# Attention: both heads of a tile multiply with v as a pair, in two column tiles of TensorE, with one PSUM bank and one evacuation

## The chip, the cores and the metric

The kernel runs on one core of a Trainium2 chip. The metric is the time of one execution on the device, in microseconds (us), and lower is better. Three runs of the kernel before gave 2673.93, 2676.56 and 2682.19 us, so the median is 2676.56 us.

## The reference, cut to what matters

The program is a stack of four layers over 1040 positions (16 meta tokens and 1024 of the sequence) with a model width of 1024: attention, mLSTM, HGRN2, attention. Layers 0 and 3 are sliding-window attention with 16 query heads of 64, four key/value heads and a window of 128 positions, computed in blocks of 128 queries against the block before and the block itself. The change touches the last line of this cut alone, in which the probabilities `p` meet the values `vv`:

```python
s = jnp.einsum('bnqhgd,bnkhd->bnhgqk', qb, kk) * (A_HD ** -0.5)
s = jnp.where(mask[None, :, None, None], s, -jnp.inf)
m = jnp.maximum(s.max(axis=-1), sink)
e = jnp.exp(s - m[..., None])
p = e / (e.sum(axis=-1) + jnp.exp(sink - m))[..., None]
o = jnp.einsum('bnhgqk,bnkhd->bnqhgd', p, vv)
...
return (o * jax.nn.silu(z.astype(jnp.float32))).astype(u.dtype) @ w_out
```

## The kernel before

Activations lie transposed: features on the 128 partitions, positions along the free axis, in three chunks of 400, 384 and 256 columns that hold blocks 0 to 3, 4 to 6, and 7 and 8. Block 0 is the 16 meta tokens alone. Projections run in three products of split operands each (`proj`, L255 and L300 for v, `proj_out`, L338), and they are most of the program.

In an attention layer (`layer_a`) the 16 heads stand in eight tiles `t` of two heads each. The two heads of a tile belong to the two key/value heads of a pair, so their 64 columns of v lie side by side: `V[kb][:, gcol : gcol + 128]` holds both. The attention of a tile is cut into *units*: block 0 alone, blocks 1 and 2, block 3, blocks 4 and 5, block 6, blocks 7 and 8, each once for each head `hh`. That makes 96 units in layer 0, and 80 in layer 3, which needs no output for the meta tokens and leaves block 0 out. Each unit goes through three steps:

- `S_step` (L583 to L623): two products of q and k for each block into a PSUM bank (L609, L610), then the mask and the maximum on VectorE (L614), the exponential with its sum on ScalarE (L618), and the division on VectorE (L620, L623) into the tile `Sm`.
- `T_step` (L625 to L640): TensorE transposes the probabilities, a 128x128 piece at a time (L634), and ScalarE copies them to SBUF as `Pt` (L640, or L637 for block 0).
- `V_step` (L642 to L660): for each block and each of its two key blocks one product in fp32 (L656), with 128 columns of v held in the array and `Pt` streamed through it. Each head has a PSUM bank of its own (`R["po", hh]`). All 128 output rows are computed, those of the other head too, and only the head's own 64 are copied out by ScalarE after the last unit of a chunk (L660):

```python
pe.matmul(po[:, q0 - c0 : q0 - c0 + nq], V[kb][:kn, gcol : gcol + P], Pt[:kn, u, ki, :nq],
          start=(ki == 0), stop=(ki == len(kbs) - 1))
```

In the trace each fp32 product of L656 stands as two weight loads and two matmuls, called passes here.

The order of TensorE's work is written out by hand. `mixers` (L662 to L673) lists the steps: in iteration k come the v step of unit k-4, the transposes of unit k-2 and the scores of unit k. So the two heads of a tile follow each other as single units. `weave` (L55) then mixes this list with the projections that are due (q of the next tile, the gate of the tile before, the output product of a pair of tiles): it takes the next element from the list that has had the smaller share of its total cost so far. The costs are TensorE nanoseconds given by hand: 427, 213 and 218 per block of a unit for the three steps, while a projection's part is its columns at 2.4 a nanosecond. `Sm` and `Pt` have two buffers each. The instructions of the other engines are ordered by priority, and those of the attention steps stand 40 ahead (`hi`, L357).

All PSUM tiles share eight banks (L144). The gate's projection for tile t (`gate_proj`, L432) multiplies into the row that L660 wrote.

Layer 2 (HGRN2) matters to the prediction for one reason: its `level_mm` (L1086 to L1108) already holds 32 columns of fp32 in the array for each product and writes the results to 32 PSUM partitions at a time, several products side by side (L1097, L1107).

Of the kernel before, what the change touches and what calls it, by code (L numbers as in the profile page):

```python
# [15 lines left out]
P = 128  # L16
# [13 lines left out]
def blk(b):  # L30
    return (0, NMETA) if b == 0 else (NMETA + P * (b - 1), P)
# [11 lines left out]
KT_LAG = 500.0  # L43
NORM_AT = (4000.0, 0.7), (5000.0, 0.5), (8000.0, 0.5)
Y_LAST, Y_EARLY, Y_AHEAD = 3, 8, 2500.0
T_LAG, V_LAG = 2, 4
PARTS = 2, 2, 2
FIRST = 0.3, 0.9, 0.3, 0.7
D_Q = 2000.0, 4000.0, 6000.0
# [21 lines left out]
def flat(groups):  # L71
    return [x for grp in groups for x in grp]
# [38 lines left out]
def hybrid_kernel(ctx: ExitStack, tc: tile.TileContext, ins, out, layers=(0, 1, 2, 3)):  # L111
    nc = tc.nc
    v, s, g, pe, sp = nc.vector, nc.scalar, nc.gpsimd, nc.tensor, nc.sync
# [11 lines left out]
    def nm(x):  # L125
        ctr[0] += 1
        return f"{x}{ctr[0]}"

    def row():
        return rpool.tile([P, T], F32, tag="r", name=nm("r"), bufs=ROWS)  # L130
# [10 lines left out]
    def small(w):  # L141
        return tpool.tile([P, w], F32, tag=f"s{w}", name=nm("s"), bufs=12 if w < 8 else 4)

    def psum(tag, bufs):  # L144
        return ps.tile([P, 512], F32, tag="p", name=nm(tag), bufs=8)
# [211 lines left out]
    def hi(fn):  # L357
        def f():
            with tc.high_priority(offset=PRIO):
                fn()  # L360

        return f
# [78 lines left out]
    def layer_a(i, j, first, last, fin):  # L441
        win, wout = ins["a_win"][j], ins["a_wout"][j]
        chunks = LAST_CHUNKS if last else CHUNKS
        R = {}
# [13 lines left out]
        order = {}  # L458
# [106 lines left out]
        V = {}  # L565
# [7 lines left out]
        def mixer(t):  # L573
            units = []
            for n, us in enumerate((((0,), (1, 2), (3,)), ((4, 5), (6,)), ((7, 8),))):
                if last and n == 0:
                    us = us[1:]
                for k, u in enumerate(us):
                    for hh in range(2):
                        units.append(dict(t=t, n=n, unit=u, hh=hh, first=k == 0, last=k == len(us) - 1))  # L580
            return units

        def mixers():  # L583
            def S_step(w):
                t = w["t"]
                mix, cons = R["mix"], R["cons"]
                unit, hh, n = w["unit"], w["hh"], w["n"]
                q, (kh, kl) = R["q", t, n][hh], R["k", t // 4][hh]
                c0 = chunks[n][0]
                nu, nq = len(unit), blk(unit[0])[1]  # L590
                head = (2 * (t // 4) + hh) * 4 + t % 4
                sink = cons[:nq, 2 + head : 3 + head]
                S = psum("pm", 2).rearrange("p (u k) -> p u k", u=2)
                w["Sm"] = Sm = mix.tile([P, 2, 257], F32, tag="Sm", name=nm("Sm"), bufs=2)
                st, den = small(2), small(2)
                w["geo"] = geo = []
                for u, b in enumerate(unit):
                    q0 = blk(b)[0]
                    if b == 0:
                        k0, kbs = 0, ((0, 0, 16),)  # L600
                    elif b == 1:
                        k0, kbs = 0, ((0, 0, 16), (1, 16, 128))
                    else:
                        k0, kbs = q0 - P, ((b - 1, 0, 128), (b, 128, 128))
                    nk = sum(z[2] for z in kbs)
                    geo.append((q0, nk, kbs))
                    kw = nk if b == 0 else 256
                    qb, kb = slice(q0 - c0, q0 - c0 + nq), slice(k0, k0 + kw)
                    pe.matmul(S[:nq, u, :kw], q[:, qb], kh[:, kb], start=True, stop=False)  # L609
                    pe.matmul(S[:nq, u, :kw], q[:, qb], kl[:, kb], start=False, stop=True)  # L610
                for u, b in enumerate(unit):
                    nk, mo = geo[u][1], {0: 128, 1: 112}.get(b, 0)
                    g.tensor_copy(Sm[:nq, u, nk : nk + 1], sink)
                    v.tensor_tensor_reduce(Sm[:nq, u, :nk], S[:nq, u, :nk], R["masks"][:nq, P + mo : P + mo + nk],  # L614
                                           -1.0, sink, ALU.add, ALU.min, st[:nq, u : u + 1])
                for u in range(nu):
                    nk = geo[u][1]
                    s.activation(Sm[:nq, u, : nk + 1], Sm[:nq, u, : nk + 1], AF.Exp, scale=-1.0,  # L618
                                 bias=st[:nq, u : u + 1], accum_out=den[:nq, u : u + 1])
                v.reciprocal(den[:nq, :nu], den[:nq, :nu])  # L620
                for u in range(nu):
                    nk = geo[u][1]
                    v.tensor_scalar(Sm[:nq, u, :nk], Sm[:nq, u, :nk], den[:nq, u : u + 1], None, op0=ALU.mult)  # L623

            def T_step(w):  # L625
                unit, geo, Sm = w["unit"], w["geo"], w["Sm"]
                nu, nq = len(unit), blk(unit[0])[1]
                pt = psum("pt", 1).rearrange("p (u k q) -> p u k q", u=2, k=2)
                w["Pt"] = Pt = R["mix"].tile([P, 2, 2, P], F32, tag="Pt", name=nm("Pt"), bufs=2)
                for u in range(nu):  # L630
                    q0, nk, kbs = geo[u]
                    for ki, (kb, ko, kn) in enumerate(kbs):
                        kn = kn if unit[u] == 0 else P
                        pe.transpose(pt[:kn, u, ki, :nq], Sm[:nq, u, ko : ko + kn], ident[:nq, :nq])  # L634
                full = [u for u in range(nu) if unit[u]]
                if not full:
                    s.copy(Pt[:NMETA, 0, 0, :nq], pt[:NMETA, 0, 0, :nq])  # L637
                else:
                    f0, f1 = full[0], full[-1] + 1
                    s.copy(Pt[:, f0:f1], pt[:, f0:f1])  # L640

            def V_step(w):  # L642
                unit, geo, Pt, hh, n, t = w["unit"], w["geo"], w["Pt"], w["hh"], w["n"], w["t"]
                nq = blk(unit[0])[1]
                if w["first"]:
                    if ("o", t) not in R:
                        R["o", t] = row()
                    R["po", hh] = psum("po", 1)
                po = R["po", hh]
                c0, cn = chunks[n]  # L650
                gcol = P * (t // 4)
                for u in range(len(unit)):
                    q0, nk, kbs = geo[u]
                    for ki, (kb, ko, kn) in enumerate(kbs):
                        kn = kn if unit[u] == 0 else P
                        pe.matmul(po[:, q0 - c0 : q0 - c0 + nq], V[kb][:kn, gcol : gcol + P], Pt[:kn, u, ki, :nq],  # L656
                                  start=(ki == 0), stop=(ki == len(kbs) - 1))
                if w["last"]:
                    hs = slice(64 * hh, 64 * hh + 64)
                    s.copy(R["o", t][hs, c0 : c0 + cn], po[hs, :cn])  # L660

            units = flat(mixer(t) for t in range(8))  # L662
            segs = [[] for _ in range(9)]
            for k in range(len(units) + V_LAG):
                seg = units[k]["t"] if k < len(units) else 8
                for lag, cost, fn in ((V_LAG, 427, V_step), (T_LAG, 213, T_step), (0, 218, S_step)):
                    if 0 <= k - lag < len(units):
                        w = units[k - lag]
                        step = [cost * len(w["unit"]), hi(lambda w=w, fn=fn: fn(w)), None]
                        segs[seg].append(step)  # L670
                        if fn is S_step and w["last"]:
                            order["S", w["t"], w["n"]] = step
            return segs  # L673

        zc = {t: gate_proj(win[12 + t], lambda t=t: R["o", t], chunks) for t in range(8)}
# [15 lines left out]
        if first:  # L691
            q0, qfin0 = qg[0]
# [4 lines left out]
        head[0].insert(0, [0.0, enter, None])  # L697
        body = []
        segs = mixers()
        for t in range(8):  # L700
            parts = [([], hang)]
# [18 lines left out]
        for t in range(1, 8):  # L720
            for n in range(3):
                at = [id(z) for z in body]
                q = at.index(id(order["q", t, n])) if id(order["q", t, n]) in at else -1
                k = at.index(id(order["S", t - 1, n]))
# [577 lines left out]
    ahead, k = 0.0, 0  # L1302
# [5 lines left out]
    k = 0  # L1308
# [125 lines left out]
```

## Time and profile before

| what | value |
|---|---|
| median of three runs | 2676.56 us |
| span of the profiled execution, first to last instruction | 2674.6 us |
| TensorE matmul busy | 2627.9 us, 98% of the span |
| VectorE busy | 1892.1 us, 71% |
| ScalarE busy | 1682.6 us, 63% |
| GpSimd busy | 151.8 us, 6% |
| v steps run in | 83 to 455 us and 2254 to 2624 us |

The span is 2.0 us shorter than the median run. In the profile's rows PE is TensorE's matmul, PEld its weight load, DVE VectorE, ACT ScalarE, POOL GpSimd and SP SyncE. A form such as `128*64 128x128` reads: rows by columns held in the array, then partitions by elements streamed through it. Matmuls overlap in the array, so the time from one start to the next says what one costs, and its duration does not.

### The profile page before, as it was taken

The numbers are of one execution on the slowest core, as the hardware profiler recorded it, in microseconds if no ns is written. First come the engines' busy times: TensorE is split into PE (matmuls) and PEld (weight loads), VectorE is DVE, ScalarE is ACT, GpSimd is POOL, SyncE is SP. The second block draws the span as 40 slices with busy tenths as digits, with TensorE's granted clock in tenths as the row PEclk, the third lists the DMA queues.
The fourth block names the chain that finished last, engine by engine and source line by source line (L and its number), as shares of the span: only waits on it lengthen the run. The fifth ranks groups of instructions, "written<-read, shape, count | busy, mean of one in ns | idle before, by whom it ended". The sixth has DMA issues, their size and how long they took to land.

```text
span 2674.6 us, 55510 instructions
## 1 busy us (share of the span) xinstructions
PE 2627.9 (98%) x20896; PEld 2535.8 (95%) x20896; DVE 1892.1 (71%) x5335; ACT 1682.6 (63%) x4301; POOL 151.8 (6%) x545
## 2 busy tenths in 40 slices
PE   7999999999999999999999999999999999999999
PEld 6999999999999999999999999899999999999999
DVE  6776767974747474747464688988888987677776
ACT  6767677565454545454544757878676857768683
POOL 1000000000000000000000000101000110000010
PEclk9999999999999999999999999999999999999999
DMA  4211111011111111111111101111111011111102
GB/s 133 60 38 49 41 49 38 17 65 56 40 56 40 56 40 56 40 56 40 56 40 49 56 26 41 33 34 33 41 33 38 29 59 49 56 43 48 46 25 87
DMA packets 74044, 126.67 MB, mean 47 GB/s; under 512 B 11552, under 2 KB 26016, under 8 KB 73776
## 3 DMA queue, kind: packets, MB, share of 16 engines
q1 hardware_dynamic: 73776, 123.13, 14.5%
q8 instruction: 165, 2.70, 0.4%
q14 instruction: 103, 0.84, 0.1%
HBM read 108.24 MB, written 4.26 MB: 42 GB/s over the span
## 4 chain that ended last, share of the span: by engine, by line
PE 82%; DVE 11%; ACT 4%; issue 1%; DMA 1%; POOL 0%; SPq 0%; DVEq 0%; ACTq 0%; POOLq 0%
PE pj L255 39%; PE pj L338 15%; PE pj L300 10%; PE po L656 4%; PE pt L634 2%; PE po L862 1%; PE pm L609 1%; PE pa L532 1%; PE pm L610 1%; PE pa L876 1%; DVE t L408 1%; PE po L864 1%; DVE ul L189 1%; DVE X L1084 1%; DVE X L1082 1%
## 5 line engine op out<-in xcount | busy, mean ns | idle before, releaser
L255 PE MATMUL pj<-uh,wh 128*128 128x384 f32 (+2 forms) x2592 | 898.5, 347 | 3.8 <-ACT uh L188 3.8
L255 PE MATMUL pj<-ul,wh 128*128 128x384 f32 (+2 forms) x2592 | 836.3, 323 | 3.1 <-DVE ul L189 2.8
L255 PE MATMUL pj<-uh,wl 128*128 128x384 f32 (+2 forms) x2592 | 834.3, 322 | 0.1
L255 PEld LDWEIGHTS pj<-uh,wh 128*128 128x128 f32 x2592 | 491.9, 190 | 23.3 <-issue 6.1
L255 PEld LDWEIGHTS pj<-ul,wh 128*128 128x128 f32 x2592 | 492.5, 190 | 14.6 <-DVE ul L189 5.9
L255 PEld LDWEIGHTS pj<-uh,wl 128*128 128x128 f32 x2592 | 491.5, 190 | 0.4 <-DVE wl L189 0.4
L300 PE MATMUL pj<-wh,uh 128*128 128x256 f32 x896 | 269.0, 300 | 0.0
L189 DVE TENSOR_TENSOR wl<-wr,wh 128x512 fp32r<-128x512 f32 x336 | 228.4, 687 | 51.9 <-ACT wh L188 48.9
L341 DVE TENSOR_TENSOR x<-x,pj 128x384 f32<-128x384 f32 (+2 forms) x480 | 235.4, 510 | 38.1 <-PE pj L338 36.4
L188 ACT CAST wh<-wr 128x512 fp32r<-128x512 f32 x337 | 202.5, 616 | 94.7 <-PE pj L338 31.8
L338 PE MATMUL pj<-yh,wh 128*128 128x384 f32 (+2 forms) x768 | 254.1, 331 | 0.0
L300 PE MATMUL pj<-wh,ul 128*128 128x256 f32 x896 | 252.8, 282 | 0.0
L300 PE MATMUL pj<-wl,uh 128*128 128x256 f32 x896 | 252.7, 282 | 0.0
L338 PE MATMUL pj<-yl,wh 128*128 128x384 f32 (+2 forms) x768 | 247.0, 322 | 3.2 <-DVE yl L189 3.2
L338 PE MATMUL pj<-yh,wl 128*128 128x384 f32 (+2 forms) x768 | 246.2, 321 | 0.0
L428 DVE SCALAR_TENSOR_TENSOR t<-pj,t 128x384 f32<-128x384 f32 (+2 forms) x192 | 98.9, 515 | 108.6 <-ACT t L427 106.6
L618 ACT ACTIVATE Sm<-Sm,s 128x257 f32<-128x257 f32 (+2 forms) x272 | 131.2, 484 | 69.3 <-DVE s L614 67.1
L300 PEld LDWEIGHTS pj<-wh,uh 128*128 128x128 f32 x896 | 169.5, 189 | 2.4
L300 PEld LDWEIGHTS pj<-wl,uh 128*128 128x128 f32 x896 | 169.7, 189 | 2.1
L429 ACT ACTIVATE t<-t 128x384 f32<-128x384 f32 (+2 forms) x240 | 117.7, 490 | 85.5 <-DVE t L428 84.7
L300 PEld LDWEIGHTS pj<-wh,ul 128*128 128x128 f32 x896 | 169.7, 189 | 0.0
L614 DVE CUSTOM_DVE_ANT_0 Sm<-pm,masks,cons 128x256 f32<-128x256 f32 (+2 forms) x272 | 115.9, 452 | 68.4 <-PE pm L610 63.7
(218 smaller groups left out, 5266.4 us busy)
## 6 DMA issues: line engine op xcount, KB each, us to landing
wr<-in_b_win SPq DMA_DIRECT2D x128, 256.0 KB, 2.7
wr<-in_a_win SPq DMA_DIRECT2D x80, 256.0 KB, 2.7
wr<-in_c_win SPq DMA_DIRECT2D x64, 256.0 KB, 2.7
r<-rowsd SPq DMA_DIRECT2D x16, 520.0 KB, 5.7
wr<-in_a_wout SPq DMA_DIRECT2D x32, 256.0 KB, 2.8
wr<-in_b_wout SPq DMA_DIRECT2D x32, 256.0 KB, 2.7
t<-t SPq DMA_DIRECT2D x96, 48.0 KB, 1.9
wr<-in_c_wout SPq DMA_DIRECT2D x16, 256.0 KB, 2.7
```

Of the source, the lines that this page charges most:

```text
L188: s.copy(h, src)
L189: v.tensor_tensor(l, src, h.bitcast(F32), op=ALU.subtract)
L255: pe.matmul(acc[:, :cn], a[:, k, :], b[:, k, c0 : c0 + cn], start=(k == 0 and i == 0), stop=(k == KT - 1 and i == 2))
L300: pe.matmul(acc[:cn, :256], a[:, k, c0 : c0 + cn], m[:, kk, :], start=(k == 0 and i == 0), stop=(k == KT - 1 and i == 2))
L338: pe.matmul(acc[:, :cn], a[:, k, mc], b, start=(k == 0 and i == 0), stop=(k == 1 and i == 2))
L341: v.tensor_tensor(x[:, m, c0 : c0 + cn], x[:, m, c0 : c0 + cn], acc[:, :cn], op=ALU.add)
L428: v.scalar_tensor_tensor(a[:, :cn], z, 0.0, a[:, :cn], op0=ALU.min, op1=ALU.subtract)
L429: s.activation(a[:, :cn], a[:, :cn], AF.Exp)
L614: v.tensor_tensor_reduce(Sm[:nq, u, :nk], S[:nq, u, :nk], R["masks"][:nq, P + mo : P + mo + nk], -1.0, sink, ALU.add, ALU.min, st[:nq, u : ...
L618: s.activation(Sm[:nq, u, : nk + 1], Sm[:nq, u, : nk + 1], AF.Exp, scale=-1.0, bias=st[:nq, u : u + 1], accum_out=den[:nq, u : u + 1])
L634: pe.transpose(pt[:kn, u, ki, :nq], Sm[:nq, u, ko : ko + kn], ident[:nq, :nq])
L656: pe.matmul(po[:, q0 - c0 : q0 - c0 + nq], V[kb][:kn, gcol : gcol + P], Pt[:kn, u, ki, :nq], start=(ki == 0), stop=(ki == len(kbs) - 1))
```

## The change

The v step now takes a pair, both heads of a unit. For each block and key block the two products follow each other: head 0's holds the 64 columns of v of its own head and writes to PSUM partitions 0 to 63, head 1's holds the next 64 columns and writes to partitions 64 to 127 of the same bank. Nothing is computed that isn't needed. One ScalarE copy of 128 partitions replaces two of 64. The number of products stays. The order of the steps changes with it: an iteration holds the v step of pair k-2, then for each head in turn the transposes of pair k-1 and the scores of pair k. The cost given to the weave for a pair's v step is 470 per block, where the two single steps had 427 each.

```diff
-T_LAG, V_LAG = 2, 4
...
-                    R["po", hh] = psum("po", 1)
-                po = R["po", hh]
+                    R["po"] = psum("po", 1)
+                po = R["po"]
...
-                        pe.matmul(po[:, q0 - c0 : q0 - c0 + nq], V[kb][:kn, gcol : gcol + P], Pt[:kn, u, ki, :nq],
-                                  start=(ki == 0), stop=(ki == len(kbs) - 1))
+                        for hh in range(2):
+                            vc = P * (t // 4) + 64 * hh
+                            pe.matmul(po[64 * hh : 64 * hh + 64, q0 - c0 : q0 - c0 + nq], V[kb][:kn, vc : vc + 64],
+                                      ws[hh]["Pt"][:kn, u, ki, :nq], start=(ki == 0), stop=(ki == len(kbs) - 1))
                 if w["last"]:
-                    hs = slice(64 * hh, 64 * hh + 64)
-                    s.copy(R["o", t][hs, c0 : c0 + cn], po[hs, :cn])
+                    s.copy(R["o", t][:, c0 : c0 + cn], po[:, :cn])
...
             units = flat(mixer(t) for t in range(8))
+            pairs = [units[k : k + 2] for k in range(0, len(units), 2)]
             segs = [[] for _ in range(9)]
-            for k in range(len(units) + V_LAG):
-                seg = units[k]["t"] if k < len(units) else 8
-                for lag, cost, fn in ((V_LAG, 427, V_step), (T_LAG, 213, T_step), (0, 218, S_step)):
...
+            for k in range(len(pairs) + 2):
+                seg = pairs[k][0]["t"] if k < len(pairs) else 8
+                v2, t1, s0 = (pairs[j] if 0 <= j < len(pairs) else None for j in (k - 2, k - 1, k))
+                if v2:
+                    put(seg, 470, V_step, v2, len(v2[0]["unit"]))
+                for hh in range(2):
+                    if t1:
+                        put(seg, 213, T_step, t1[hh], len(t1[hh]["unit"]))
+                    if s0:
+                        step = put(seg, 218, S_step, s0[hh], len(s0[hh]["unit"]))
...
```

More of the change, by code (lines that the diff above doesn't have):

```diff
@@ L640, in T_step, with V_step @@
                     s.copy(Pt[:, f0:f1], pt[:, f0:f1])
-            def V_step(w):
-                unit, geo, Pt, hh, n, t = w["unit"], w["geo"], w["Pt"], w["hh"], w["n"], w["t"]
+            def V_step(ws):
+                w = ws[0]
+                unit, n, t = w["unit"], w["n"], w["t"]
                 nq = blk(unit[0])[1]
@@ L647, in V_step @@
                         R["o", t] = row()
-                    R["po", hh] = psum("po", 1)
-                po = R["po", hh]
+                    R["po"] = psum("po", 1)
+                po = R["po"]
                 c0, cn = chunks[n]
-                gcol = P * (t // 4)
                 for u in range(len(unit)):
-                    q0, nk, kbs = geo[u]
+                    q0, nk, kbs = w["geo"][u]
                     for ki, (kb, ko, kn) in enumerate(kbs):
                         kn = kn if unit[u] == 0 else P
-                        pe.matmul(po[:, q0 - c0 : q0 - c0 + nq], V[kb][:kn, gcol : gcol + P], Pt[:kn, u, ki, :nq],
-                                  start=(ki == 0), stop=(ki == len(kbs) - 1))
+                        for hh in range(2):
+                            vc = P * (t // 4) + 64 * hh
+                            pe.matmul(po[64 * hh : 64 * hh + 64, q0 - c0 : q0 - c0 + nq], V[kb][:kn, vc : vc + 64],
+                                      ws[hh]["Pt"][:kn, u, ki, :nq], start=(ki == 0), stop=(ki == len(kbs) - 1))
@@ L658, in V_step, with put @@
                 if w["last"]:
-                    hs = slice(64 * hh, 64 * hh + 64)
-                    s.copy(R["o", t][hs, c0 : c0 + cn], po[hs, :cn])
+                    s.copy(R["o", t][:, c0 : c0 + cn], po[:, :cn])
             units = flat(mixer(t) for t in range(8))
+            pairs = [units[k : k + 2] for k in range(0, len(units), 2)]
             segs = [[] for _ in range(9)]
-            for k in range(len(units) + V_LAG):
-                seg = units[k]["t"] if k < len(units) else 8
-                for lag, cost, fn in ((V_LAG, 427, V_step), (T_LAG, 213, T_step), (0, 218, S_step)):
[L667 to L672, printed above, removed]
+            def put(seg, cost, fn, w, nu):
+                step = [cost * nu, hi(lambda: fn(w)), None]
+                segs[seg].append(step)
+                return step
@@ new lines, in mixers @@
+            for k in range(len(pairs) + 2):
[8 more added lines that the diff above has]
+                        step = put(seg, 218, S_step, s0[hh], len(s0[hh]["unit"]))
+                        if s0[hh]["last"]:
+                            order["S", s0[hh]["t"], s0[hh]["n"]] = step
```

## The prediction

> **What bounds the kernel now.** First the page's busy times, then the busy time by windows for two stretches of attention where the steps stand closest (columns: window, length, then busy time with count of PE, PEld, DVE, ACT, POOL, the granted clock, DMA share, GB/s).
>
> ```profile
> span 2674.6 us, 55510 instructions
> PE 2627.9 (98%) x20896; PEld 2535.8 (95%) x20896; DVE 1892.1 (71%) x5335; ACT 1682.6 (63%) x4301; POOL 151.8 (6%) x545
> ```
> ```profile
> 387.00:424.00 37.00, 37.00 (x270) 35.45 (x269) 26.64 (x92) 30.28 (x85) 3.73 (x19) 1.00 0.09 24
> 2543.00:2575.00 32.00, 32.00 (x230) 30.98 (x229) 22.51 (x73) 24.20 (x65) 2.88 (x13) 1.00 0.17 50
> ```
>
> TensorE is never out of work in these stretches and its clock is whole; ScalarE reaches 82% (30.28 of 37.00) and VectorE 72%. So in the attention layers time is TensorE time: what a v step no longer takes there shortens the run, as long as its input comes in time. I count it by the groups with shapes kept apart.
>
> ```profile
> L656 PE MATMUL po<-Pt,v 128*128 128x128 f32 x1024 | 140.8, 275 | 0.7 <-ACT v L270 0.7
> L656 PE MATMUL po<-Pt,v 16*128 16x16 f32 x32 | 6.3, 268 | 0.0
> L640 ACT COPY Pt<-pt 128x512 f32<-128x512 f32 x96 | 55.9, 582 | 12.3 <-PE pt L634 10.4 <-PE pm L610 0.8
> L640 ACT COPY Pt<-pt 128x256 f32<-128x256 f32 x64 | 23.4, 366 | 10.3 <-PE pt L634 10.1
> ```
>
> Each v step has one such copy before it, so there are 96 steps of two blocks (8 passes each), 64 of one block (4 passes; 96x8 + 64x4 = 1024) and 32/2 = 16 of the meta block. The change makes pairs: 48, 32 and 8.
>
> **What a v step costs today.** The busy column won't do, since matmuls overlap; starts will. The timeline of TensorE around one step of two blocks:
>
> ```profile
> 302.91 0.34 PE L338 MATMUL pj<-yl,wh 128*128 128x400 f32 x1
> 303.10 0.34 PE L338 MATMUL pj<-yh,wl 128*128 128x400 f32 x1
> 303.28 1.05 PE L656 MATMUL po<-Pt,v 128*128 128x128 f32 x8
> 304.09 0.43 PE L338 MATMUL pj<-yh,wh 128*128 128x400 f32 x1
> 304.35 0.35 PE L338 MATMUL pj<-yl,wh 128*128 128x400 f32 x1
> ```
>
> From 303.10 to 304.35 are 1.25 us, of which two projection matmuls take 0.18 each (303.10 to 303.28). Eight passes cost 0.89, or 0.111 each, and going in and out costs nothing. A pair of two blocks costs 1.78 us today, a pair of one block 0.89. The meta step is different:
>
> ```profile
> 82.96 0.28 PE L255 MATMUL pj<-uh,wl 128*128 128x256 f32 x1
> 83.17 0.39 PE L656 MATMUL po<-Pt,v 16*128 16x16 f32 x2
> 83.48 0.45 PE L255 MATMUL pj<-uh,wh 128*128 128x400 f32 x1
> 83.78 0.35 PE L255 MATMUL pj<-ul,wh 128*128 128x400 f32 x1
> ```
>
> 0.82 us less 0.12 (256 columns, by proportion) and 0.18: 0.52 for two tiny passes. An operand of 16 rows breaks the stream on both sides. A pair costs 1.04.
>
> **What it will cost.** No 128x64 operand occurs in the trace, but the HGRN2 layer holds 128x32 operands and writes each to its own 32 PSUM partitions, which is the same thing in quarters. One such visit (the long row of other passes and some single ones left out; 112 passes in all), then its first four passes in a narrower window, and the group that gives the last pass's length:
>
> ```profile
> 1814.54 0.34 PE L255 MATMUL pj<-uh,wl 128*128 128x384 f32 x1
> 1814.81 0.50 PE L1097 MATMUL pm<-X 128*32 128x64 f32 x15
> ...
> 1815.17 0.92 PE L1107 MATMUL pm<-X 128*32 128x32 f32 x76
> ...
> 1815.92 0.34 PE L1107 MATMUL pm<-Q,X 128*32 128x32 f32 x15
> 1816.19 0.45 PE L255 MATMUL pj<-uh,wh 128*128 128x384 f32 x1
> 1816.48 0.34 PE L255 MATMUL pj<-ul,wh 128*128 128x384 f32 x1
> ```
> ```profile
> 1814.81 0.25 PE L1097 MATMUL pm<-X 128*32 128x64 f32 x2
> 1814.81 0.31 PE L1097 MATMUL pm<-X 128*32 128x64 f32 x4
> L1107 PE MATMUL pm<-Q,X 128*32 128x32 f32 x512 | 11.4, 200 | 0.0
> ```
>
> Three readings. *Rate*: the first four passes lie in two tiles of the array; the second two end 0.06 us after the first two (0.31 against 0.25). A pass of 64 columns costs 0.056 by itself (half of 0.111), so two run in the time of one. The later rows, four tiles deep, agree: 76 passes of 32 columns, 0.028 each by proportion, would take 2.1 us one by one, and the row lasts 0.92. *In*: 1814.54 to 1814.81 is 0.27, a matmul of 384 columns costs 0.17: 0.09 lost to emptying the array. The first weights load in the open as well: 0.03 for 32 columns and 0.05 for 64 by the 0.111 that a full operand's pass gives as a bound for 128 columns. *Out*: the last pass started at 1815.92 + 0.34 - 0.20 = 1816.06; to 1816.48 are 0.42, of which 0.17 are the full matmul and 0.03 the pass: 0.21 lost. Together 0.35 us each time the array is divided and made whole again. The bounds are 0.30 (the small load hidden) and 0.52, the whole meta visit; I take 0.35, the row of the same kind.
>
> So a pair of two blocks needs 8 slots of 0.111, two passes side by side in each, plus 0.35: 1.24 instead of 1.78, a gain of 0.54. One block: 0.44 + 0.35 = 0.79 instead of 0.89, a gain of 0.10. Meta: one visit, two slots, about 0.6 instead of 1.04, a gain of 0.44. The sum is 48 x 0.54 + 32 x 0.10 + 8 x 0.44 = 25.9 + 3.2 + 3.5 = **32.6 us gained**. Nearly half of the 57 us that halving the passes offers (512 slots of 0.111) goes into dividing the array 80 times.
>
> A page's figure for the rate: the Trainium skill (TensorE: Matmul & The Clock Gate, Part 3, Measured speedup vs the span model) has three column tiles at 2.38 times one; an estimate from it, 0.79 of ideal, would stretch a slot to 0.14 and cost 15 us of the gain. The rows above show no such loss.
>
> **What the new order costs.** Today a v step follows its own transposes after a scores step and a whole further iteration. Now head 1's transposes are followed by one scores step and then by the v step that needs them. The trace has this neighbourhood already, only that the v step in it belongs to older units:
>
> ```profile
> 403.43 0.60 PE L634 MATMUL pt<-const,Sm 128*128 128x128 f32 x4
> 403.79 0.37 PE L609 MATMUL pm<-r,qs 128*128 128x256 f32 x1
> 404.74 0.59 ACT L640 COPY Pt<-pt 128x512 f32<-128x512 f32 x1
> 405.15 1.05 PE L656 MATMUL po<-Pt,v 128*128 128x128 f32 x8
> ```
>
> The copy ends at 405.33, 0.18 us after the v step that would need it began. I took this difference for all 176 transpose steps; the first and the last are
>
> ```profile
> 77.97 0.17 PE L634 MATMUL pt<-const,Sm 16*16 16x16 f32 x1 [1.70 <-DVE s L620]
> 78.17 0.16 ACT L637 COPY Pt<-pt 16x16 f32<-16x16 f32 x1 [0.54 <-PE pt L634]
> 2616.64 0.60 PE L634 MATMUL pt<-const,Sm 128*128 128x128 f32 x4
> 2617.79 0.57 ACT L640 COPY Pt<-pt 128x512 f32<-128x512 f32 x1
> 2619.19 1.05 PE L656 MATMUL po<-Pt,v 128*128 128x128 f32 x8
> ```
>
> (the first's next v step is the meta one at 83.17). Of 176, 45 copies end late, by 29 us together; head 1's are half of it, 15 us. The distance grows, though: the filler between two steps goes by their costs, a pair's now sum to 1332 per block (470 + 2x213 + 2x218) instead of 1716 (2 x 858) with the filler unchanged, so each unit of cost carries 1.29 times the filler; with the steps' own shorter time the distance is about 1.2 times. Then 31 are late, by 21 us, and half is **10 us of waiting on TensorE**, which holds up every projection behind it in TensorE's order. Bounds: 0 (ScalarE, with fewer evacuations, gets to the copies sooner) and 15. The other distance, from scores to their transposes, goes from 1503 cost units (218+427+213+218+427) to 1119 (218+213+218+470) x 1.29 = 1444, 4% less. Today's waits there and on `Pt` are
>
> ```profile
> PE pt L634 <- DVE Sm L623: 2.4, 3, 0.9
> PE po L656 <- ACT v L270: 0.7, 1, 0.7
> ```
>
> (total, times, longest; none on `Pt`), so I put 2 us more there, 0 to 5. The evacuations, one of 128 partitions for two of 64, are off the path while ScalarE has 18% idle, and the freed PSUM bank has no wait to remove: both count nothing.
>
> Sum: 32.6 - 10 - 2 = 20.6 us. The profiled execution would take 2654.0 us of span; it lies 2.0 us under the median of the runs, so I forecast 2676.6 - 20.6 = **2656 us**. About 0.3%, 8 us, is what a measurement can tell from no change.
>
> **The rivals.** *No new wait*: the copies keep pace. All 32.6 us stay: 2644. For it: none is late on today's spacing with an iteration more, and ScalarE gets lighter; against it: the 45 late ones.
>
> *The wait decides*: the v step needs both heads' copies, and head 1's lies behind ScalarE's queue. Each wait is paid in full at the pair's v step. From 32.6/88 = 0.37 us per pair on average the gain is gone; at 0.6, 53 us or five times the late sum, the loss is 20 us: 2697. Against it: even at today's unscaled spacing the mean is 15/88 = 0.17.
>
> *Weights in the open*: within a tile the next weights might have to wait for the pass before. Each slot then takes 0.111 + 0.05 = 0.16; two blocks cost 1.64 (gain 0.14), one block 1.00 (loss 0.11), meta as before: 6.7 - 3.5 + 3.5 = 7 us, and with the waits -5: 2682. The Trainium skill says as much (TensorE: Matmul & The Clock Gate, Part 3, The mechanism): a weight load overlaps matmuls in flight only where the row group differs, and column tiles share theirs. The trace disagrees by the 0.06 us between pairs of 64-column passes: with a 0.03 load in the open it would be 0.08.
>
> *The tiles don't overlap*: a pair keeps its 16 passes and adds the 0.35: 80 x 0.35 - 3.5 + 12 = 37 us slower, 2713. The 76 passes in 0.92 us speak against it.
>
> **How the numbers follow.** The forecast has 0.63, no new wait 0.20, the deciding wait 0.08, open weights 0.07, no overlap 0.02. The forecast's own range: division 0.30 to 0.45 over 88 visits gives +4 to -9 us, waits of 5 to 18 us instead of 12 give +7 to -6, so 2645 to 2670. With "no new wait" at its upper part the range is **2642 to 2669**; what is left out is the other three cases and little of the first two. Faster by over 8 us: nearly all of the first two, 0.82. Within 0.3%: the forecast's worst end and part of open weights and the deciding wait, 0.11. Slower by over that: 0.07.
>
> **What would show it.** Right: L656 with 1024 passes of form 128*64; a two-block visit from the matmul before to the second after of about 1.6 us (1.24 + 2 x 0.18), 0.27 going in; passes starting in near pairs 0.11 apart; new waits of L656 on L640, some 10 us, at short spacing. Wrong: passes 0.11 apart singly, pairs 0.16 apart, or L656's waits above 30 us. ScalarE's L660 halves in count without moving the end.

## The result and the profile after

The changed kernel takes 2644.82 us (median of four runs, 2644.08 to 2647.87), the kernel before 2676.70 beside it: a ratio of 0.9885, with a 95% interval from 0.9869 to 0.9901. By the medians that is 31.9 us less. The profiled execution, itself of 2644.08 us, has a span 32.3 us shorter than the one of before. The page of the changed kernel (its lines are numbered one to ten off from before; the v step's product is L657 now):

```profile
span 2642.3 us, 55429 instructions
PE 2592.4 (98%) x20896; PEld 2472.1 (94%) x20896; DVE 1888.3 (71%) x5335; ACT 1656.6 (63%) x4253; POOL 155.8 (6%) x545
```

TensorE still has 20896 matmuls and still fills 98% of the span. What has changed is how they lie. First the groups of the v step's products, shapes kept apart, then TensorE's timeline around one pair of two blocks:

```profile
L657 PE MATMUL po<-Pt,v 128*64 128x128 f32 x1024 | 76.7, 281 | 1.9 <-ACT Pt L639 1.8
L657 PEld LDWEIGHTS po<-Pt,v 128*64 128x64 f32 x1024 | 55.9, 136 | 19.5 <-issue 5.9 <-ACT Pt L639 3.4 <-ACT Sm L617 2.6
```
```profile
303.69 0.34 PE L337 MATMUL pj<-yl,wh 128*128 128x384 f32 x1
303.87 0.34 PE L337 MATMUL pj<-yh,wl 128*128 128x384 f32 x1
304.14 1.09 PE L657 MATMUL po<-Pt,v 128*64 128x128 f32 x16
305.16 0.45 PE L337 MATMUL pj<-yh,wh 128*128 128x384 f32 x1
305.44 0.34 PE L337 MATMUL pj<-yl,wh 128*128 128x384 f32 x1
```

There are 1024 passes as before, but a pass's mean is no shorter (281 ns against 275): durations of overlapping matmuls show nothing of the gain. The starts do. From 303.87 to 305.44 are 1.57 us, less two projection matmuls of 0.175: 1.22 for 16 passes, where two steps of eight took 1.78. Going in takes 0.27 (303.87 to 304.14) instead of 0.18. The passes lie in pairs. The busy time by windows, of this line's instructions alone, counts eight passes in the first 0.48 us of the step (columns: window, length, PE busy with its count, PEld busy with its count, clock, DMA share, GB/s):

```profile
304.13:304.61 0.48, 0.47 (x8) 0.47 (x10) 1.00 0.00 0
```

I added up what all v steps cost in this way, from the start of the matmul before to the second start after, less those two matmuls. Before, it is 126.2 us over 176 steps, and now 92.8 over 88: 33.4 us less. The same sum for the transposes goes from 67.2 to 69.1 us; the middle (median) of a transpose step has not changed, so this is waiting. So the two steps account for 31.5 of the span's 32.3 us. TensorE's waits at these steps (total, times, longest):

```profile
PE pt L633 <- DVE Sm L622: 3.9, 6, 1.2
...
PE po L657 <- ACT Pt L639: 1.8, 4, 0.7
```

The new wait, on the copy of the transposes, is there, and it is small.

### The profile page after: what moved, and what is told of

Same layout as the page of the kernel before. It is cut to its first block, busy times and chain, and to the rows that moved or that the text cites. A ratio compares the mean times of both kernels' runs of the same rounds, so it can differ in the third digit from the quotient of the medians.

```text
span 2642.3 us, 55429 instructions
## 1 busy us (share of the span) xinstructions
PE 2592.4 (98%) x20896; PEld 2472.1 (94%) x20896; DVE 1888.3 (71%) x5335; ACT 1656.6 (63%) x4253; POOL 155.8 (6%) x545
## 4 chain that ended last, share of the span: by engine, by line
PE 81%; DVE 11%; ACT 5%; DMA 1%; issue 1%; SPq 0%; POOL 0%; DVEq 0%; ACTq 0%; POOLq 0%
PE pj L254 39%; PE pj L337 16%; PE pj L299 10%; PE po L657 3%; PE pt L633 2%; PE po L872 1%; PE pa L531 1%; DVE t L407 1%; PE pa L886 1%; PE pm L608 1%; DVE ul L188 1%; PE po L874 1%; PE pm L609 1%; PE pj L295 1%; DVE X L1094 1%
## 5 line engine op out<-in xcount | busy, mean ns | idle before, releaser
L254 PEld LDWEIGHTS pj<-uh,wh 128*128 128x128 f32 x2592 | 490.4, 189 | 33.4 <-issue 16.6
L254 PEld LDWEIGHTS pj<-ul,wh 128*128 128x128 f32 x2592 | 491.0, 189 | 14.3 <-DVE ul L188 6.0
L187 ACT CAST yh<-r 128x384 fp32r<-128x384 f32 (+2 forms) x120 | 57.2, 479 | 162.7 <-PE pj L337 139.5
```

The lines of the kernel that those rows point to most:

```text
L187: s.copy(h, src)
L254: pe.matmul(acc[:, :cn], a[:, k, :], b[:, k, c0 : c0 + cn], start=(k == 0 and i == 0), stop=(k == KT - 1 and i == 2))
```

## The experiments

My theory: the gain is two tiles of the array at work at once, less a price for each time the array is divided and made whole; the new order costs waits, the single evacuation nothing. The rivals: order, evacuation and the freed bank bring part of it; the division is cheap or the alternation needless; the waits are what limits the gain.

**The new order without the tiles.** Each head's products have all 128 columns again, head 0's first, with a bank and an evacuation each:

```diff
+                for hh in range(2):
+                    po = R["po", hh]
...
+                            pe.matmul(po[:, q0 - c0 : q0 - c0 + nq], V[kb][:kn, gcol : gcol + P],
+                                      ws[hh]["Pt"][:kn, u, ki, :nq], start=(ki == 0), stop=(ki == len(kbs) - 1))
```

> The new order of the steps with the old products: a pair's v step takes head 0's products with all 128 columns of v into one bank, then head 1's into another, with two evacuations of 64 partitions. Theory (the gain is the array's two tiles; the order costs waits, the evacuation nothing): a pair of two blocks is back at 1.78 us, and the waits of the new order are all that differs from before: 2678 to 2683 us by the V visits measured after the change (2 us more excess than before), 2689 if my 12 us of waits were right. Rival (the order or the single evacuation carries part of the gain): below 2668 us.

Measured: 2673.34 us, a ratio to the kernel before of 0.9994 (0.9981 to 1.0007). No difference. The rival is out: by the interval no more than about 5 us of the 31.9 could come from the order. My own range, 2678 to 2683, was missed too, since the waits did not grow. Its waits at the two steps:

```profile
PE pt L633 <- DVE Sm L622: 4.1, 6, 1.2
...
PE pt L633 <- DVE s L619: 0.9, 1, 0.9
...
PE po L657 <- ACT Pt L639: 0.8, 2, 0.5
```

V steps sum to 123.0 us, 3.2 less than before, of which 2.9 are the meta pairs': two steps of 16 rows in one visit cost 0.74 us instead of 2 x 0.52, 2.4 us over eight pairs, and the rest is less waiting. Transposes sum to 68.4, 1.2 more. The run does not measure the changed kernel's waits, though: head 0's products come first here and give head 1's copy up to 0.89 us more. By this run's trace 16 of head 1's copies end after the v step's start, 6.6 us together, and yet the v steps wait less than before. What the new order costs together with the tiles is read from the changed kernel's own steps, below.

**The tiles without pairs.** The old order and single heads, each with its own 64 columns and its own 64 partitions:

```diff
-                        pe.matmul(po[:, q0 - c0 : q0 - c0 + nq], V[kb][:kn, gcol : gcol + P], Pt[:kn, u, ki, :nq],
+                        pe.matmul(po[64 * hh : 64 * hh + 64, q0 - c0 : q0 - c0 + nq],
+                                  V[kb][:kn, gcol + 64 * hh : gcol + 64 * hh + 64], Pt[:kn, u, ki, :nq],
```

> The old order with single heads, but each head's products hold only its own 64 columns of v and write to its own 64 PSUM partitions, so that the array is divided for every v step and no two passes can lie side by side. Theory (dividing and restoring the array costs 0.35 us, and one tile runs at the old 0.111 us a pass): 160 visits of 0.35 more, 56 us slower than before, 2733 us. Rival 1 (the division is nearly free for 64 columns): 2677 us. Rival 2 (half the weight columns make a single pass cheaper): below 2677 us.

Measured: 2723.10 us, a ratio of 1.0184 (1.0162 to 1.0206), 46.7 us slower, 10 us less than I expected. Around one step of two blocks:

```profile
311.43 0.34 PE L338 MATMUL pj<-yh,wl 128*128 128x400 f32 x1
311.70 1.09 PE L656 MATMUL po<-Pt,v 128*64 128x128 f32 x8
312.72 0.46 PE L338 MATMUL pj<-yh,wh 128*128 128x400 f32 x1
313.02 0.34 PE L338 MATMUL pj<-yl,wh 128*128 128x400 f32 x1
```

311.43 to 313.02 less 2 x 0.18 is 1.23, and the middle of all 96 such steps is 1.21, against 0.89 before: 0.32 more. Steps of one block rise from 0.45 to 0.78, 0.33 more. So the division has one price, whatever the step holds, and it lies a little under my 0.35. Eight passes in one tile cost what sixteen in two tiles cost in the changed kernel (1.22): the second head's cost nothing more. All v steps sum to 175.2 us, 49.0 more than before; the meta steps alone became cheaper (0.41 from 0.52).

**Grouped instead of alternating.** The loop over heads goes outside:

```diff
-                for u in range(len(unit)):
-                    q0, nk, kbs = w["geo"][u]
-                    for ki, (kb, ko, kn) in enumerate(kbs):
-                        kn = kn if unit[u] == 0 else P
-                        for hh in range(2):
+                for hh in range(2):
+                    for u in range(len(unit)):
+                        q0, nk, kbs = w["geo"][u]
+                        for ki, (kb, ko, kn) in enumerate(kbs):
+                            kn = kn if unit[u] == 0 else P
```

> As the changed kernel, but a pair's v step issues all of head 0's products first and then all of head 1's, with no alternation. Theory A (TensorE takes matmuls in program order, so only neighbours overlap): a pair of two blocks needs nearly 16 slots of 0.111 and the 0.35, 2.0 us instead of 1.22; 57 us less the overlap at the seam (one slot) of each visit, about 45 to 55 us slower than the changed kernel, 2690 to 2700 us. Theory B (each tile is fed on its own, far ahead in the program): no change, 2645 us.

Measured: 2667.93 us, a ratio of 0.9967 (0.9957 to 0.9977): 23 us slower than the changed kernel, half of what theory A said, and B is out. The timeline shows why, first a pair of one block, then one of two:

```profile
303.79 0.34 PE L337 MATMUL pj<-yh,wl 128*128 128x400 f32 x1
304.06 0.66 PE L657 MATMUL po<-Pt,v 128*64 128x128 f32 x8
304.66 0.45 PE L337 MATMUL pj<-yh,wh 128*128 128x400 f32 x1
304.94 0.34 PE L337 MATMUL pj<-yl,wh 128*128 128x400 f32 x1
...
312.86 0.34 PE L337 MATMUL pj<-yh,wl 128*128 128x384 f32 x1
313.13 1.58 PE L657 MATMUL po<-Pt,v 128*64 128x128 f32 x16
314.64 0.45 PE L337 MATMUL pj<-yh,wh 128*128 128x384 f32 x1
314.92 0.34 PE L337 MATMUL pj<-yl,wh 128*128 128x384 f32 x1
```

The one-block pair, four passes of head 0 and then four of head 1, still costs 0.79 us (304.94 - 303.79 - 0.36): full overlap without alternation. The two-block pair, eight and then eight, costs 1.71. In its first 0.48 us four passes begin where the changed kernel has eight:

```profile
313.12:313.60 0.48, 0.47 (x4) 0.47 (x5) 1.00 0.00 0
```

After these four, single and 0.11 apart, a second stream joins 6 ns after the fifth, and the last four are single again. Each stream lasts as long as a head alone. The rows do not name a head. That the second stream is head 1's I take from its first weight load, which waits for the semaphore of the `Pt` copies, and from its first pass, which is as long (0.32 us) as the first of a step. A late copy is not what sets the moment: in 47 of the 48 two-block pairs the second stream begins 0.49 us after the first. So head 1's first pass, ninth in the kernel's order, began together with the fifth, ahead of head 0's remaining three: in this run TensorE did not start matmuls strictly in the kernel's order where their tiles differ, but it reached only some four passes ahead. What sets that reach is not shown. The Trainium skill (TensorE: Matmul & The Clock Gate, Part 3, The mechanism) has matmuls start and end in strict program order; by that rule the one-block pair would have overlapped at its seam alone, some 1.1 us (an estimate: seven slots of 0.109 and the division's 0.33), and this run says otherwise.

**Alternating by block**, four passes of a head at a time, tests that reach:

```diff
-                    for ki, (kb, ko, kn) in enumerate(kbs):
-                        kn = kn if unit[u] == 0 else P
-                        for hh in range(2):
+                    for hh in range(2):
+                        for ki, (kb, ko, kn) in enumerate(kbs):
+                            kn = kn if unit[u] == 0 else P
```

> The changed kernel, but within a v step the products alternate by block: head 0's two key blocks (four passes), then head 1's two, then the next block. In the grouped run head 1's first pass started with head 0's fifth, and steps of one block overlapped fully. Theory (TensorE starts a matmul on a free tile up to about four passes ahead of its turn): the four passes in the way are within reach, so the steps cost 1.22 and 0.78 us as in the changed kernel, 2645 us within 2 us. Rival (it overlaps only what comes next, and the grouped run's start was an accident of the tail): a two-block step near 1.7 us, 20 us slower, 2665 us.

Measured: 2644.30 us, a ratio of 0.9885 (0.9869 to 0.9901), the changed kernel's. A pair of two blocks is 0.05 us longer in the timeline, 390.48 to 392.10 less 2 x 0.175 is 1.27, since its last passes lie half a slot apart; 48 x 0.05 is under what the runs can tell.

```profile
390.48 0.34 PE L254 MATMUL pj<-uh,wl 128*128 128x384 f32 x1
390.75 1.14 PE L657 MATMUL po<-Pt,v 128*64 128x128 f32 x16
391.82 0.44 PE L254 MATMUL pj<-uh,wh 128*128 128x384 f32 x1
392.10 0.34 PE L254 MATMUL pj<-ul,wh 128*128 128x384 f32 x1
```

**Two evacuations.**

```diff
-                    s.copy(R["o", t][:, c0 : c0 + cn], po[:, :cn])
+                    for hs in (slice(0, 64), slice(64, 128)):
+                        s.copy(R["o", t][hs, c0 : c0 + cn], po[hs, :cn])
```

> As the changed kernel, but the evacuation is two ScalarE copies of 64 partitions out of the one bank instead of one of 128: 48 copies more of about 0.46 us, 22 us of ScalarE. Theory (off the path): 2645 us within 2 us. Rival (ScalarE's queue sets the copies of the transposes, and with them the v step): 5 to 10 us slower, 2650 to 2655 us.

Measured: 2643.81 us, a ratio of 0.9884 (0.9865 to 0.9904), the same as the changed kernel. The single evacuation brings nothing that these runs can tell, as ScalarE's idle share suggested.

**Another order in an iteration**, both heads' transposes and then both heads' scores, to move the waits on purpose:

```diff
                 for hh in range(2):
                     if t1:
                         put(seg, 213, T_step, t1[hh], len(t1[hh]["unit"]))
+                for hh in range(2):
                     if s0:
```

> The changed kernel with another order in an iteration: v step, both heads' transposes, then both heads' scores. The transposes come 650 cost units ahead of their v step instead of 431, the scores 906 ahead of their transposes instead of 1119. Theory 1 (the wait is what a fixed delay of the other engines leaves over a changed distance, the way the prediction worked it out): by the changed kernel's trace the late divisions grow from 1 to 14 us and the late copies of the transposes fall from 4.6 to 2 us: about 10 us slower, 2655 us. Theory 2 (that method overstates, since the order of ScalarE and VectorE and their backlog follow the new spacing): within 3 us of 2645.

Measured: 2651.92 us, a ratio of 0.9915 (0.9896 to 0.9933), 7.1 us above the changed kernel, with intervals that just overlap. Waits at the transposes:

```profile
PE pt L633 <- DVE Sm L622: 7.9, 12, 1.1
...
PE pt L633 <- ACT Pt L639: 2.2, 2, 1.3
```

The transposes sum to 77.6 us, 8.5 more (theory 1: 13), the v steps to 88.8, 4.0 less (theory 1: 2.6). A net of 4.5 us by the trace, whose run was the fastest of the four (2647.79), and 7 by the runs, between the theories: waits do follow the distances, but at the transposes by about two thirds of what unchanged delays would give.

**Fewer divisions.** If a division costs 0.33 us whatever it holds, steps should be long. Units cut across the chunks make four of two blocks for each tile:

```diff
-            for n, us in enumerate((((0,), (1, 2), (3,)), ((4, 5), (6,)), ((7, 8),))):
...
+            for u in ((0,), (1, 2), (3, 4), (5, 6), (7, 8))[1 if last else 0 :]:
```

The scores then pick q, and the v step its bank, by each block's chunk.

> The changed kernel with its units cut across the chunks: blocks 1 and 2, 3 and 4, 5 and 6, 7 and 8 (and the meta block by itself), so that a tile has four v steps of two blocks instead of three of two blocks and two of one; a chunk's evacuation follows the step that holds its last block. Theory (each division of the array costs 0.33 us whatever it holds): the 32 pairs of one block become 16 of two, 16 divisions less, 5.3 us faster than the changed kernel, 2639 to 2640 us; fewer, longer steps add no wait worth 2 us. Rival (the waits grow, since two evacuations and a longer wait for q stand at the seams): no gain or slower, 2645 us or more.

Measured: 2630.52 us, a ratio to before of 0.9831 (0.9813 to 0.9850): 46 us under the kernel before and 14.3 under the changed one, faster than both, and 9 us below the 2639 to 2640 that I expected. The v steps sum to 85.1 us, 7.7 less than in the changed kernel: 5.3 for the divisions, the rest less waiting. The transposes fell by 6.4 us to 62.7, which I had not expected. TensorE's waits there are nearly gone:

```profile
PE po L658 <- ACT Pt L640: 1.1, 2, 0.9
...
PE pt L634 <- DVE s L620: 0.9, 1, 0.9
```

The 3.9 us that the transposes waited for the division in the changed kernel are off the list. I take it that steps of one length leave an even distance between scores and transposes, where a short step used to follow a long one; that is argued, and no run separates it. So of the 14.3 us the sums of the two steps hold 14.1, but only 5.3 are the divisions that the run was made for.

## Why the prediction was right, point by point

The kernel was forecast at 2656 us within 2642 to 2669, and measured at 2644.8: the sign and the mechanism hold, and the time came out where the rival without new waits stood (2644). The forecast itself missed by 11 us, and the range held because it took that rival in: the waits were put 8 us too high and the gross gain 3 us too low.

*What bounds the kernel*: right. TensorE's time in the attention layers is the run's time: 33.4 us less in the v steps and 1.9 more in the transposes make 31.5 of the 32.3 by which the span fell.

*The gross gain*, 32.6 us: near, measured 35.5. By the middles over all steps, a pair of two blocks gained 1.79 - 1.22 = 0.57 (0.54 forecast), one block 0.89 - 0.78 = 0.11 (0.10), the meta pair 1.03 - 0.42 = 0.61 (0.44). 48, 32 and 8 times these, before rounding, are 27.1 + 3.5 + 4.9 = 35.5 us, of which 2.2 went into waits at the v steps. Half of the 2.9 us that were missing is the meta pair, which had been given a round 0.6 us. Two passes lie side by side at 0.109 us a slot. The price of the division, 0.35 from the HGRN2 layer's narrower operands, is 0.32 to 0.33.

*The waits of the new order*, 10 + 2 us: this is the term that was mis-sized. At the v steps the excess over the middles (the sum over all steps less what it would be if each took its shape's middle) rose by 2.2 us (3.8 to 6.0), at the transposes by 1.9: 4.1 us, a third. The distance was right: from the start of head 1's last transpose to its v step 2.15 us in the middle, where 1.2 times the old neighbourhood's 1.70 gives 2.04. The count of late copies was not: 10, by 4.6 us. Nor were head 1's half of the old ones: the trace of before gives head 1 25 of the 45, 18.2 of the 29 us, and at 1.2 times the distance 18 of the 31 with 13.5 us, so the method overstates by more than its 10 us say. What failed was to keep the delays of the old order. The copy ended 1.03 us after the start of the last transpose in the middle and 2.11 at the ninth tenth before, and 0.95 and 1.67 after. For head 1's copies alone, the ones that count, the middle even rose, from 1.03 to 1.13, and the ninth tenth fell from 2.25 to 1.71: it is the long delays that went. The two-evacuations run has 0.98 and 1.55 over both heads, so it is not the lighter ScalarE. That the other engines' own order follows the new spacing fits, also with the run that swapped transposes and scores, but nothing here isolates it, and the cause stays open.

*The wait decides*: out. It needed 0.37 us of waiting in a pair to take the gain away; the waits at the v steps rose by 2.2/88 = 0.025.

*Weights in the open* and *no overlap*: both out. The rule of the Trainium skill that I had as a rival (TensorE: Matmul & The Clock Gate, Part 3, The mechanism: weight loads overlap matmuls in flight only on other row groups, though the same section also lets a load into a background weight buffer go ahead) would have made slots of 0.16; they are 0.109. The first slot of a step alone is 0.05 longer, as put. The Trainium skill's figure for three column tiles (TensorE: Matmul & The Clock Gate, Part 3, Measured speedup vs the span model: 2.38 times one, by estimate 0.79 of ideal) is not what two tiles do here: at 0.109 us for a slot of two passes they reach all of it.

*The evacuation and the bank at nothing*: right for the evacuation (0.9884 against 0.9885). The bank by itself wasn't tried.

## What to carry to other kernels

Two fp32 products of 64 output rows, put in two column tiles of TensorE and issued within four passes of each other, ran in the time of one; but every stretch in a divided array cost about 0.33 us at its two ends. So gather such products into long stretches, and do not divide the array for a stretch in which one tile works alone: here that cost 46.7 us. A wait that a reordering threatens was overstated when the old delays were laid over the new distances, here by a factor of about three. A run of the new order without the rest of the change is a cheap test of it, but only if it keeps the order of the products inside a step as well. And where the array's time is the bound, look at starts, not at durations or busy shares.

## What the runs showed of the hardware beyond that

A matmul can start ahead of its turn: with eight passes of one tile in front, the other tile's first pass started with the fifth of them, and with four in front it started at once (13 ns later in the one-block pair shown). Operands of 16 rows break the stream at both ends too: 0.52 us for two tiny passes before, 0.74 for four in one visit.
